# First layer's mixer projections as single fp32 products, and the log steps of the state space laid out as one run per partition

## The chip, the cores and the metric

The kernel runs on one core of a Trainium2 chip. The metric is the device time of one execution in microseconds, the median over runs. Its work is spread over TensorE (PE in the profile; PEld is its weight load), VectorE (DVE), ScalarE (ACT), GpSimd (POOL) and the DMA queues, one of which is fed by SyncE (SP).

## The reference

Two layers over 512 tokens of width 1024. Each layer is a mixer and an expert stage:

```python
xn = rms_norm(h, norm1_g[l])
proj = xn @ w_in[l]                       # 1024 x 2056: u, q, k, v (512 each), f (8)
y_ssm = s5_mixer(u, lambda, log_dt, b, c, ...)     # 32 groups of 64 complex states
y_att = fox_attention(q, k, v, f + fox_b[l])
h = h + concat(rms_norm(y_ssm), rms_norm(y_att)) @ w_o[l]
h = h + peer_ffn(rms_norm(h, norm2_g[l]), ...)     # top 16 of 16384 experts, 8 heads
```

In `s5_mixer`, `dt = exp(log_dt)` has one value per group (32 per layer), and from it, lambda, b and c come the tables of the scan. All of it is float32.

## The kernel before

Tokens lie in 4 blocks of 128 (TB), the width in 8 blocks of 128 (KD). A program order is written in Python; a scheduler with a timeline of its own then puts the instructions of each engine in a fixed order, and buffers and semaphores are derived from that. So a change in one place may move others.

**Projections.** `norm_T` (L239) normalises each token block, transposes it on PE (L256) and writes it in two parts: `x1`, rounded to fp32r by ACT (L259), and the rest `x2` by DVE (L260). `stream` (L178) loads blocks of `w_in` of 512 KB on SP's queue into 5 buffers called `raw` (L157) and `wsplit` (L161) splits each the same way: `hi` on ACT (L166), `lo` on POOL or DVE (L167). `mm3` (L198) then forms a product as three fp32r matmuls: hi x1, hi x2, lo x1 (L200 to L202). `proj_T` (L211) does that for a 128-column block of weights: two halves of 256 tokens, 8 steps of k each. In the mixer there are 13 such blocks (4 for u, 1 for f, 4 for q, 4 for k) and then v, with the weights as the moving operand of 512 columns: 32 products. In the first layer `lo` is made on POOL for the blocks with `i % 4 != 3` and on DVE for the rest and for v.

**Tables of the scan.** `s5_prep` (L265) loads lambda, `log_dt`, b, c and d on SP's queue (L279 to L291), takes the exponential of `log_dt` on ACT (L293), and works out sines and cosines (L304 to L323), powers (L328 to L333, L378 to L380), and for each of four groups of heads three tables, with transposes (L459) and small products (L471) on PE, and part of the work on POOL. They go out to DRAM (`s5p`, L415, L438, L462, L482) and come back in `s5` (L586). For the first layer this runs at the start, between the projections. For the second it is woven into the first layer's expert stage: its loads stand in SP's queue between those of expert weights.

**Scan, attention, output.** `s5` (L570) runs four groups: products L594, DVE work L600 to L621, products L625 to L627, a GELU on ACT, transposes L633. Then come the gate (`glu`, first product L644), attention (L677 to L691) and the output projection.

**Expert stage.** Norm, routing and gate tables; then 116 of 128 blocks of expert weights `peer_uT` are loaded, split and multiplied as above (`u_stage`), with results stored to DRAM (`ad`); then the second tables. Near the start of the u blocks, ACT's queue also loads gates (`g<-gd`) and results (`ar<-ad`) ahead.

The lines of `s5_prep` that load the log steps, and their host side (L1090):

```python
bass.AP(tensor=ld.tensor, offset=ld.offset + l * 2 * NPR + g, ap=[[0, 64], [2, NPR]])   # NPR = 16
o["log_dt"] = c(f("ssm_log_dt"))
```

Each of two loads fills 64 partitions with the same 16 values, read from every second element.

Of the kernel before, what the change touches and what calls it, by code (L numbers as in the profile page):

```python
# [9 lines left out]
F32R = mybir.dt.float32r  # L10
# [3 lines left out]
AF = mybir.ActivationFunctionType  # L14
OP = mybir.AluOpType
# [4 lines left out]
L, S, D = 2, 512, 1024  # L20
TB = S // 128
KD = D // 128
NPR = 16
# [21 lines left out]
class Net:  # L45
# [136 lines left out]
    def stream_rest(s, specs, depth, ahead, raws):  # L182
        out = {}
        n = len(specs)

        def fetch(i):
            for k in range(i, min(i + ahead, n)):
                if k not in raws:
                    raws[k] = s.wload(*specs[k][:2])
            for k in range(i, min(i + depth, n)):  # L190
                if k not in out:
                    out[k] = s.wsplit(raws[k], specs[k][2] if len(specs[k]) > 2 else False)

        for i in range(n):
            fetch(i)
            yield out.pop(i)
# [14 lines left out]
    def proj_T(s, p, wh, wl):  # L211

        for hf in range(2):
            po = s.toks(p[:, 256 * hf:256 * hf + 256])
            for k in range(KD):
                bs = slice(2 * hf, 2 * hf + 2)
                s.mm3(po, wh[:, k], wl[:, k], s.x1[:, bs, k], s.x2[:, bs, k], k == 0, k == 7)


# [16 lines left out]
        nc.vector.reciprocal(r, q)  # L236
        return r

    def norm_T(s, gain, gb, xt, pt, order=range(TB)):  # L239

        nc = s.nc
        nc.scalar.dma_start(gb, bass.AP(tensor=gain.tensor, offset=gain.offset + s.l * D, ap=[[0, 128], [1, D]]))
        x1 = s.k("x1", [TB, KD, 128], F32R)
        x2 = s.k("x2", [TB, KD, 128], F32R)
        for b in order:
            ssq = s.k("ssq", [16], bufs=4)
            xn = s.t(xt, [D], bufs=2) if xt else s.k("raw", [1024], bufs=5)
            with s.tc.high_priority(offset=NORM):
                nc.scalar.activation(xn, s.h[:, b], AF.Square, accum_out=ssq[:, 0:1])
                r = s.rstd(ssq[:, 0:1], 1, D)  # L250
                s.normed = s.sqrt
                s.scaled = nc.vector.scalar_tensor_tensor(xn, s.h[:, b], r, gb, op0=OP.mult, op1=OP.mult)
            for q in range(2):
                p = s.p(pt)
                for k in range(4):
                    nc.tensor.transpose(p[:, k * 128:(k + 1) * 128], xn[:, (4 * q + k) * 128:(4 * q + k + 1) * 128],  # L256
                                        s.ident)
                pk = p.rearrange("p (k t) -> p k t", k=4)
                nc.scalar.activation(x1[:, b, 4 * q:4 * q + 4], pk, AF.Copy)  # L259
                nc.vector.tensor_tensor(x2[:, b, 4 * q:4 * q + 4], pk, x1[:, b, 4 * q:4 * q + 4], op=OP.subtract)  # L260
        s.x1, s.x2 = x1, x2
        return xn


    def s5_prep(s, l, engs, ptag, bufs):  # L265

        nc, a = s.nc, s.a
# [6 lines left out]
        def new():  # L274
            idx[0] += 1
            return sm[:, idx[0] - 1]
# [4 lines left out]
        ld = a["log_dt"]  # L281
        for g in range(2):
            nc.sync.dma_start(dt[g * 64:(g + 1) * 64],
                              bass.AP(tensor=ld.tensor, offset=ld.offset + l * 2 * NPR + g,
                                      ap=[[0, 64], [2, NPR]]))
        bc = s.t("pbc", [4, NPR, 16])
        for i, n in enumerate(("b_re", "b_im", "c_re", "c_im")):
            nc.sync.dma_start(bc[:, i], a[n][l])
# [69 lines left out]
        nr, q = new(), new()  # L358
# [127 lines left out]
    def mixer(s):  # L486
        nc, a, l = s.nc, s.a, s.l
# [1 line left out]

        qa = [s.t(f"q{i}", [2, S]) for i in range(4)]  # L490
        wv = a["w_in"][l].rearrange("(k p) c -> p k c", p=128)
        specs = [(wv[:, :, 128 * cb:128 * cb + 128], [8, 128], l == 0 and i % 4 != 3)
                 for i, cb in enumerate(list(range(0, 4)) + [16] + list(range(4, 12)))]
        specs += [(wv[:, 2 * i:2 * i + 2, 1536:2048], [2, 512]) for i in range(4)]
        ws = s.stream(specs, pre=2)
        if l == 0:
            early = s.phase("prep")
# [1 line left out]
            prep = s.s5_prep(0, (nc.vector, nc.gpsimd), "pt", 2)  # L499
            next(prep)  # L500
            s.sb = s.mix
        s.norm_T(a["norm1_g"], s.k("hn", [D]), None, "pt", (3, 0, 1, 2) if l else range(TB))
        if l == 0:
            s.small_loads()
        x1, x2 = s.x1, s.x2

        us = []
        for qd in range(4):
            wh, wl = next(ws)
# [13 lines left out]
        wh, wl = next(ws)  # L523
# [19 lines left out]
        with s.phase("s5"):  # L543
            s.s5(us, gT)
            ka = [s.tm(f"k{i}", [2, S]) for i in range(4)]
            for i in range(4):
                nc.gpsimd.memset(ka[i][64:66], 1.0)
                nc.scalar.dma_start(ka[i][65:66], f0[2 * i:2 * i + 2])
            for cb in range(4):
                wh, wl = next(ws)  # L550
                p = s.p("pj")
                s.proj_T(p, wh, wl)
                for hh in range(2):
                    nc.scalar.activation(qa[cb][0:64, hh], p[64 * hh:64 * hh + 64], AF.Copy, scale=0.125)
            for cb in range(4):
                wh, wl = next(ws)
                p = s.p("pj")
                s.proj_T(p, wh, wl)
                for hh in range(2):
                    v.tensor_copy(ka[cb][0:64, hh], p[64 * hh:64 * hh + 64])  # L560
            vv = s.tm("v", [TB, 512])
            pv = [s.p("pj") for _ in range(4)]
            for i in range(4):
                wh, wl = next(ws)
                for kk in range(2):
                    k = 2 * i + kk
                    for b in range(4):
                        s.mm3(pv[b], x1[:, b, k], x2[:, b, k], wh[:, kk], wl[:, kk], k == 0, k == 7)
            for b in range(4):
                s.evac(vv[:, b], pv[b])  # L570
        with s.phase("att"):
            s.glu(gT)
            op = s.out_proj()
# [497 lines left out]
def layout(inp):  # L1071

    import numpy as np
    c = np.ascontiguousarray
    f = lambda n: np.asarray(inp[n])
    o = {}
# [10 lines left out]
    o["fox_b"] = c(f("fox_b_f").T)  # L1087
    st = lambda n: c(f(n).reshape(L, 16, 2, 64).transpose(0, 2, 3, 1).reshape(L, 128, 16))
    o["lam_re"], o["lam_im"] = st("ssm_lambda_re"), st("ssm_lambda_im")
    o["log_dt"] = c(f("ssm_log_dt"))  # L1090
    sb = lambda n: c(f(n).reshape(L, 16, 2, 64, 16).transpose(0, 2, 3, 1, 4).reshape(L, 128, 16, 16))
    o["b_re"], o["b_im"] = sb("ssm_b_re"), sb("ssm_b_im")
    sc = lambda n: c(f(n).reshape(L, 16, 2, 16, 64).transpose(0, 2, 4, 1, 3).reshape(L, 128, 16, 16))
# [36 lines left out]
```

## Time and profile before

| what | us |
|---|---|
| median of 3 runs | 3337.83 (3333.64 to 3341.49) |
| the profiled execution | 3333.71 |
| its span | 3331.9 |
| TensorE busy | 3068.3 (92% of the span) |
| VectorE / GpSimd / ScalarE busy | 2607.7 / 1630.1 / 1450.8 |
| mean granted TensorE clock | 0.962 of full speed |

The span runs from the first to the last instruction; the rest of the execution's own time, 1.8 us, lies outside it. Times in the rows are counted from the span's start. Matmuls are pipelined: the time of one in a row is from its start to its end, and what it costs in a stream is the step from one start to the next. An fp32 matmul of the program stands as two PE instructions in the trace. The first layer's mixer runs from 0 to about 321 us, its expert stage to about 1730; the second layer follows in the same way.

### The profile page before, as it was taken

How to read it: one execution, taken by the hardware profiler on the slowest of the kernel's cores; microseconds unless marked ns; L12 is line 12 of the kernel's file. 1: busy time of each engine (PE TensorE's matmuls, PEld its weight loads, DVE VectorE, ACT ScalarE, POOL GpSimd, SP SyncE). 2: the span in 40 equal slices, each digit the busy share in tenths (PEclk: the TensorE clock that was granted, in tenths of full speed). 3: DMA queues.
4: the chain of work that ended last, by engine and by line, in shares of the span. 5: the costliest groups of instructions: out<-in, count | busy, mean ns of one | idle time of the engine just before them, and what ended most of it. 6: DMA issues, size and time to landing. Idle time of an engine off the chain costs nothing.

```text
span 3331.9 us, 45931 instructions
## 1 busy us (share of the span) xinstructions
PE 3068.3 (92%) x16418; PEld 2708.6 (81%) x16418; DVE 2607.7 (78%) x4907; ACT 1450.8 (44%) x2591; POOL 1630.1 (49%) x890
## 2 busy tenths in 40 slices
PE   6889988899979998999999999888999999999998
PEld 5856978888969877778879669878989998788887
DVE  7775699988745789888877556999886658888887
ACT  3344322378823343333343433334887333333333
POOL 3400276656569555454420003766756884544452
PEclk8989988899989999999999999889999999999999
DMA  5612276657778988999974123766767999899996
GB/s 153 216 44 64 100 246 227 212 217 277 261 247 293 335 313 306 315 335 336 321 239 145 51 64 114 248 221 210 260 245 280 306 311 332 308 354 340 339 337 217
DMA packets 395446, 811.12 MB, mean 243 GB/s; under 512 B 30768, under 2 KB 236592, under 8 KB 392144
## 3 DMA queue, kind: packets, MB, share of 16 engines
q1 hardware_dynamic: 140448, 326.23, 28.6%
q0 software_dynamic: 73728, 268.47, 22.8%
q10 hardware_dynamic: 181040, 213.48, 19.1%
q8 instruction: 129, 2.11, 0.3%
q14 instruction: 101, 0.83, 0.1%
HBM read 693.19 MB, written 114.82 MB: 243 GB/s over the span
## 4 chain that ended last, share of the span: by engine, by line
PE 50%; DVE 22%; issue 9%; DMA 8%; ACT 3%; POOL 2%; ACTq 1%; POOLq 0%; DVEq 0%; SPq 0%
PE pb L908 15%; PE pc L908 7%; DMA ru<-in_peer_u_dram,idx 6%; PE pa L202 3%; PE pa L200 3%; PE pa L201 3%; DVE ru L932 2%; DVE t L862 2%; DVE h L935 2%; PE pb L872 2%; PE pc L202 2%; PE pc L200 2%; PE pc L201 2%; DVE t L817 2%; DVE lo L167 1%
## 5 line engine op out<-in xcount | busy, mean ns | idle before, releaser
L167 POOL TENSOR_TENSOR lo<-raw,hi 128x1024 fp32r<-128x1024 f32 x306 | 822.0, 2693 | 940.4 <-ACT hi L166 898.0
L166 ACT ACTIVATE hi<-raw 128x1024 fp32r<-128x1024 f32 x578 | 610.2, 1057 | 683.8 <-issue 167.4
L908 PE MATMUL pb<-hi,cc 128*128 128x512 f32 x2048 | 608.2, 399 | 16.9 <-DVE cc L898 9.1
L932 DVE SCALAR_TENSOR_TENSOR ru<-ru,hn 128x1024 f32<-128x1024 f32 x256 | 393.7, 1539 | 209.3 <-DMA ru<-in_peer_u_dram,idx 209.1
L908 PEld LDWEIGHTS pb<-hi,cc 128*128 128x128 f32 x2048 | 386.2, 190 | 111.9 <-DVE cc L898 12.4
L167 DVE TENSOR_TENSOR lo<-raw,hi 128x1024 fp32r<-128x1024 f32 x272 | 337.9, 1244 | 128.8 <-ACT hi L166 126.2
L921 POOL DMA_INDIRECT rv<-in_peer_v_dram,idx x256 | 372.3, 1454 | 129.6 <-issue 49.2
L921 POOL DMA_INDIRECT ru<-in_peer_u_dram,idx x256 | 384.0, 1500 | 91.3 <-DVE ru L932 31.3
L202 PE MATMUL pa<-x,lo 128*128 128x384 f32 x1120 | 389.4, 348 | 17.1 <-POOL lo L167 16.5
L200 PE MATMUL pa<-x,hi 128*128 128x384 f32 x1120 | 388.4, 347 | 11.8 <-ACT hi L166 11.7
L201 PE MATMUL pa<-x,hi 128*128 128x384 f32 x1120 | 387.2, 346 | 0.0
L935 DVE SCALAR_TENSOR_TENSOR h<-rv,gc,h 128x1024 f32<-128x1024 f32 x256 | 377.2, 1473 | 10.0 <-DMA rv<-in_peer_v_dram,idx 5.2
L200 PE MATMUL pc<-x,hi 128*128 128x384 f32 x928 | 327.3, 353 | 32.2 <-ACT hi L166 32.2
L202 PE MATMUL pc<-x,lo 128*128 128x384 f32 x928 | 326.7, 352 | 16.8 <-POOL lo L167 16.6
L908 PE MATMUL pb<-lo,cc 128*128 128x512 f32 x1024 | 325.5, 399 | 9.9 <-DVE lo L167 9.8
L201 PE MATMUL pc<-x,hi 128*128 128x384 f32 x928 | 324.7, 350 | 0.0
L908 PE MATMUL pc<-hi,cc 128*128 128x512 f32 x1024 | 323.9, 397 | 0.0
L933 ACT ACTIVATE gc<-gc 128x1 f32<-128x1 f32 x256 | 51.4, 201 | 527.6 <-DVE ru L932 451.7
L862 DVE TENSOR_TENSOR t<-io,idt 128x2048 f32<-128x2048 f32 x96 | 259.5, 2713 | 5.7 <-PE pb L872 5.6
L872 PE MATMUL pb<-small,t 128*128 128x128 f32 x1536 | 221.8, 288 | 36.0 <-ACT small L866 21.5
L872 PEld LDWEIGHTS pb<-small,t 128*128 128x128 f32 x1536 | 210.5, 198 | 48.6 <-ACT small L866 30.6
L897 ACT ACTIVATE cc<-c 128x384 fp32r<-128x384 f32 x256 | 132.9, 519 | 254.8 <-DVE c L895 191.2
(329 smaller groups left out, 5974.4 us busy)
## 6 DMA issues: line engine op xcount, KB each, us to landing
raw<-in_peer_uT_dram SPq DMA_DIRECT2D x256, 512.0 KB
raw<-in_peer_v_dram SPq DMA_DIRECT2D x256, 512.0 KB
gd<-t ACTq DMA_DIRECT2D x24, 2048.0 KB
g<-gd ACTq DMA_DIRECT2D x64, 768.0 KB
ad<-ao ACTq DMA_DIRECT2D x232, 192.0 KB
ar<-ad ACTq DMA_DIRECT2D x58, 768.0 KB
raw<-in_w_in_dram SPq DMA_DIRECT2D x34, 512.0 KB
s5p<-pE ACTq DMA_DIRECT2D x16, 512.0 KB
```

What stands on the lines that cost most here:

```text
L166: s.nc.scalar.activation(hi, raw, AF.Copy)
L167: ins = eng.tensor_tensor(lo, raw, hi, op=OP.subtract)
L200: mm(ps, lh, rh, start=start, stop=False)
L201: mm(ps, lh, rl, start=False, stop=False)
L202: mm(ps, ll, rh, start=False, stop=stop)
L862: v.tensor_tensor(oh, s.iota[:, None, None, :].to_broadcast([128, 2, 8, 128]), idT[:, 0:2, t0:t0 + 8, None].to_broadcast([128, 2, 8, 128]) ...
L872: nc.tensor.matmul(p[:, t], oh[:, 1, 4 * f + t], o2[:, 4 * f + t], start=True, stop=True)
L897: on_act = nc.scalar.activation(ch, c[:, 0], AF.Copy)
L908: s.nc.tensor.matmul(s.pv[tb][hf], x[:, sl], y[:, 512 * hf:512 * hf + 512], start=(first and e == 0), stop=(last and e == 2))
L921: nc.gpsimd.indirect_dma_start(out=o, out_offset=None, in_=a[n], in_offset=off)
L932: v.scalar_tensor_tensor(ru, ru, 1.0, s.hn, op0=OP.mult, op1=OP.mult, accum_out=c[:, 0:1])
L935: v.scalar_tensor_tensor(acc, rv, c[:, 2:3], acc, op0=OP.mult, op1=OP.add)
```

## The change

In the first layer the weights of the mixer's projections and the normalised tokens are no longer split. `stream` hands out the raw weight buffer itself when the third entry of a spec is None, `norm_T` with `split=False` writes one fp32 tile on ACT, and the products are single fp32 matmuls. The second layer, the output projection and the expert stage keep the split. And `log_dt` is transposed on the host, so that each partition reads 16 values that lie next to each other (64 bytes).

```diff
@@ stream_rest
-                    out[k] = s.wsplit(raws[k], specs[k][2] if len(specs[k]) > 2 else False)
+                    how = specs[k][2] if len(specs[k]) > 2 else False
+                    out[k] = (s.view(*raws.pop(k)), None) if how is None else s.wsplit(raws[k], how)
@@ proj_T
+                if wl is None:
+                    s.nc.tensor.matmul(po, wh[:, k], s.x[:, bs, k], start=(k == 0), stop=(k == 7))
+                    continue
                 s.mm3(po, wh[:, k], wl[:, k], s.x1[:, bs, k], s.x2[:, bs, k], k == 0, k == 7)
@@ norm_T
-                nc.scalar.activation(x1[:, b, 4 * q:4 * q + 4], pk, AF.Copy)
-                nc.vector.tensor_tensor(x2[:, b, 4 * q:4 * q + 4], pk, x1[:, b, 4 * q:4 * q + 4], op=OP.subtract)
+                if split:
+                    ...
+                else:
+                    nc.scalar.activation(s.x[:, b, ks], pk, AF.Copy)
@@ s5_prep
-                              bass.AP(tensor=ld.tensor, offset=ld.offset + l * 2 * NPR + g,
-                                      ap=[[0, 64], [2, NPR]]))
+                              bass.AP(tensor=ld.tensor, offset=ld.offset + (2 * l + g) * NPR,
+                                      ap=[[0, 64], [1, NPR]]))
@@ mixer
-        specs = [(wv[:, :, 128 * cb:128 * cb + 128], [8, 128], l == 0 and i % 4 != 3)
-                 for i, cb in enumerate(list(range(0, 4)) + [16] + list(range(4, 12)))]
-        specs += [(wv[:, 2 * i:2 * i + 2, 1536:2048], [2, 512]) for i in range(4)]
+        how = False if l else None
+        specs = [(wv[:, :, 128 * cb:128 * cb + 128], [8, 128], how) for cb in [0, 1, 2, 3, 16] + list(range(4, 12))]
+        specs += [(wv[:, 2 * i:2 * i + 2, 1536:2048], [2, 512], how) for i in range(4)]
@@ mixer, v
-                        s.mm3(pv[b], x1[:, b, k], x2[:, b, k], wh[:, kk], wl[:, kk], k == 0, k == 7)
+                        if wl is None:
+                            nc.tensor.matmul(pv[b], s.x[:, b, k], wh[:, kk], start=(k == 0), stop=(k == 7))
+                        else:
+                            s.mm3(pv[b], s.x1[:, b, k], s.x2[:, b, k], wh[:, kk], wl[:, kk], k == 0, k == 7)
@@ layout
-    o["log_dt"] = c(f("ssm_log_dt"))
+    o["log_dt"] = c(f("ssm_log_dt").reshape(L, NPR, 2).transpose(0, 2, 1))
```

The scheduler orders the first layer's mixer anew. Behind it the engines' orders are as before but for a few neighbours that change places.

On PE before, the scan's first products (L594, `wb` is a table that came back from DRAM, `u` the first projection) stand behind all 13 projection blocks and part of v (`pj` written from `hi` and `lo` with 512 columns):

```order
L202 MATMUL pj_1756<-hi_1759,x_26_125 128x512
L200 MATMUL pj_1753<-hi_1759,x_25_124 128x512
L201 MATMUL pj_1753<-lo_1760,x_25_124 128x512
L202 MATMUL pj_1753<-hi_1759,x_26_125 128x512
L200 MATMUL pj_1754<-hi_1759,x_25_124 128x512
L201 MATMUL pj_1754<-lo_1760,x_25_124 128x512
L202 MATMUL pj_1754<-hi_1759,x_26_125 128x512
L594 MATMUL p_161_1034<-u_287,wb_1028 128x128
L594 MATMUL p_162_1035<-u_287,wb_1028 128x128
```

On PE now (the same products are L607, a projection is L219) they stand inside the last two blocks of k:

```order
L219 MATMUL pj_1210<-x_25_124,raw_1166 128x256 x16
L219 MATMUL pj_1231<-x_25_124,raw_1187 128x256 x7
L607 MATMUL p_148_841<-u_238,wb_835 128x128
L607 MATMUL p_149_842<-u_238,wb_835 128x128
...
L219 MATMUL pj_1231<-x_25_124,raw_1187 128x256 x9
L219 MATMUL pj_1252<-x_25_124,raw_1208 128x256 x5
L607 MATMUL p_162_905<-u_266,wb_899 128x128
```

Ahead of the first L594 there were 208 products of projections and 14 products of v; ahead of the first L607 there are 183 products, and the other 25 and nearly all of v come between the scan's groups.

On ACT before, at the start, the splits (`hi`) stand between the copies of the transposed tokens (`x`) and the exponential of the log steps (L293, `psm` is the tile of the small vectors):

```order
L166 ACTIVATE hi_228<-raw_99 128x1024
L234 ACTIVATE rs_q_203<-rs_m_201 128x1
L259 ACTIVATE x_25_124<-pt_160 128x512
L166 ACTIVATE hi_232<-raw_101 128x1024
L259 ACTIVATE x_25_124<-pt_167 128x512
L293 ACT_TABLE_LOAD
L293 ACTIVATE psm_107<-psm_107 128x16
L259 ACTIVATE x_25_124<-pt_184 128x512
L166 ACTIVATE hi_296<-raw_226 128x1024
L296 ACTIVATE psm_107<-psm_107 128x16
```

On ACT now (L272 is the copy, L304 the exponential):

```order
L272 ACTIVATE x_25_124<-pt_157 128x512
L238 ACTIVATE rs_q_196<-rs_m_194 128x1
L272 ACTIVATE x_25_124<-pt_163 128x512
L304 ACT_TABLE_LOAD
L304 ACTIVATE psm_107<-psm_107 128x16
L307 ACTIVATE psm_107<-psm_107 128x16
L323 ACT_TABLE_LOAD
L323 ACTIVATE psm_107<-psm_107 128x16 x2
L272 ACTIVATE x_25_124<-pt_179 128x512
```

The splits are gone, and the copies of the last two token blocks stand behind both sines (L323).

## Rows read from the trace of the kernel before

**Rows 1.** Page, part 2: PE busy in tenths, 40 slices of 83.3 us.

```profile
PE   6889988899979998999999999888999999999998
```

**Rows 2.** Windows, first layer: us, then busy us (count) per engine, clock, DMA.

```profile
15.60:33.50 17.90, 4.45 (x19) 3.91 (x19) 3.67 (x8) 2.71 (x3) 5.52 (x2) 0.71 0.13 30
33.50:150.40 116.90, 100.49 (x759) 97.30 (x760) 91.97 (x256) 42.71 (x83) 56.43 (x47) 0.94 0.62 192
150.40:202.50 52.10, 42.50 (x243) 37.62 (x243) 44.75 (x87) 10.71 (x13) 0.34 (x3) 0.84 0.38 127
```

**Rows 3.** Timeline of ACT: start us, us, instruction, idle before it and its end.

```profile
32.22 1.28 ACT L293 ACT_TABLE_LOAD   x1 [15.19 <-DMA psm<-in_log_dt_dram]
```

**Rows 4.** DMA packets between 14 and 30 us.

```profile
DMA packets 1701, 0.01 MB, mean 0 GB/s; under 512 B 1701, under 2 KB 1701, under 8 KB 1701
```

**Rows 5.** Timeline of PE: start us, us, instruction; two neighbours each time.

```profile
17.50 0.41 PE L200 MATMUL pj<-x,hi 128*128 128x256 f32 x1
17.71 0.41 PE L201 MATMUL pj<-x,hi 128*128 128x256 f32 x1
...
134.56 0.28 PE L200 MATMUL pj<-x,hi 128*128 128x256 f32 x1
134.68 0.28 PE L201 MATMUL pj<-x,hi 128*128 128x256 f32 x1
...
140.70 0.39 PE L200 MATMUL pj<-hi,x 128*128 128x512 f32 x1
140.93 0.39 PE L201 MATMUL pj<-lo,x 128*128 128x512 f32 x1
```

**Rows 6.** Chain of waits, 0 to 420 us: start us, us, group.

```profile
124.54 1.70 PE pt L471 x16
...
150.62 1.57 PE p L594 x14
...
202.73 6.87 PE pt L644 x16
```

**Rows 7.** Groups by line, 0 to 202.5: count | busy us, mean ns.

```profile
L167 POOL TENSOR_TENSOR lo<-raw,hi 128x1024 fp32r<-128x1024 f32 x10 | 28.6, 2864 | 33.7 <-ACT hi L166 24.8 <-ACT rs_q L234 8.8
...
L167 DVE TENSOR_TENSOR lo<-raw,hi 128x1024 fp32r<-128x1024 f32 x10 | 12.7, 1269 | 5.9 <-ACT hi L166 5.5 <-issue 0.4
...
L166 ACT ACTIVATE hi<-raw 128x1024 fp32r<-128x1024 f32 x20 | 21.1, 1056 | 43.0 <-PE pj L202 16.5 <-DVE pEa L378 10.3 <-PE pj L201 7.3
```

**Rows 8.** Timeline of DVE and POOL, 40 to 90 us.

```profile
40.67 0.83 DVE L318 TENSOR_TENSOR psm<-psm 128x16 f32<-128x16 f32 x1 [3.12 <-ACT psm L312]
...
82.18 0.67 DVE L425 TENSOR_TENSOR pP<-pT,half 128x512 f32<-128x512 f32 x1
...
84.35 4.48 POOL L167 TENSOR_TENSOR lo<-raw,hi 128x1024 fp32r<-128x1024 f32 x1 [5.73 <-ACT hi L166]
...
86.55 2.82 DVE L425 TENSOR_TENSOR pP<-pT,half 128x512 f32<-128x512 f32 x1
```

**Rows 9.** Windows, expert stage: first layer, and the same place in the second.

```profile
930.00:966.00 36.00, 12.20 (x53) 10.55 (x51) 7.78 (x8) 6.98 (x12) 9.47 (x5) 0.70 0.56 186
...
2588.00:2624.00 36.00, 30.41 (x158) 29.78 (x157) 27.65 (x22) 14.99 (x25) 29.57 (x16) 0.91 0.93 318
```

**Rows 10.** Timeline of the SP queue, 921 to 961 us.

```profile
921.89 7.95 SPq L283 DMA_DIRECT2D psm<-in_log_dt_dram  x2
...
935.16 3.16 SPq L157 DMA_DIRECT2D raw<-in_peer_uT_dram  x1
...
960.36 0.86 SPq L157 DMA_DIRECT2D raw<-in_peer_uT_dram  x2
```

**Rows 11.** Waits, PE (906 to 970), SP (915 to 965): total, times, longest.

```profile
PE pc L200 <- ACT hi L166: 20.8, 2, 12.4
...
SPq L288 <- DMA g<-gd: 9.1, 1, 9.1
...
SPq L288 <- DMA ar<-ad: 7.2, 1, 7.2
```

More of the change, by code (lines that the diff above doesn't have):

```diff
@@ L187, in fetch @@
             for k in range(i, min(i + ahead, n)):
-                if k not in raws:
+                if k not in raws and k not in out:
                     raws[k] = s.wload(*specs[k][:2])
@@ L237, in rstd, with norm_T @@
         return r
-    def norm_T(s, gain, gb, xt, pt, order=range(TB)):
+    def norm_T(s, gain, gb, xt, pt, order=range(TB), split=True):
         nc = s.nc
         nc.scalar.dma_start(gb, bass.AP(tensor=gain.tensor, offset=gain.offset + s.l * D, ap=[[0, 128], [1, D]]))
-        x1 = s.k("x1", [TB, KD, 128], F32R)
-        x2 = s.k("x2", [TB, KD, 128], F32R)
+        if split:
+            s.x1 = s.k("x1", [TB, KD, 128], F32R)
+            s.x2 = s.k("x2", [TB, KD, 128], F32R)
+        else:
+            s.x = s.k("x1", [TB, KD, 128])
         for b in order:
@@ L258, in norm_T @@
                 pk = p.rearrange("p (k t) -> p k t", k=4)
-                nc.scalar.activation(x1[:, b, 4 * q:4 * q + 4], pk, AF.Copy)
-                nc.vector.tensor_tensor(x2[:, b, 4 * q:4 * q + 4], pk, x1[:, b, 4 * q:4 * q + 4], op=OP.subtract)
-        s.x1, s.x2 = x1, x2
+                ks = slice(4 * q, 4 * q + 4)
+                if split:
+                    nc.scalar.activation(s.x1[:, b, ks], pk, AF.Copy)
+                    nc.vector.tensor_tensor(s.x2[:, b, ks], pk, s.x1[:, b, ks], op=OP.subtract)
+                else:
+                    nc.scalar.activation(s.x[:, b, ks], pk, AF.Copy)
         return xn
@@ L501, in mixer @@
             s.sb = s.mix
-        s.norm_T(a["norm1_g"], s.k("hn", [D]), None, "pt", (3, 0, 1, 2) if l else range(TB))
+        s.norm_T(a["norm1_g"], s.k("hn", [D]), None, "pt", (3, 0, 1, 2) if l else range(TB), split=l > 0)
         if l == 0:
             s.small_loads()
-        x1, x2 = s.x1, s.x2
         us = []
@@ L567, in mixer @@
                     for b in range(4):
-                        s.mm3(pv[b], x1[:, b, k], x2[:, b, k], wh[:, kk], wl[:, kk], k == 0, k == 7)
+                        if wl is None:
+                            nc.tensor.matmul(pv[b], s.x[:, b, k], wh[:, kk], start=(k == 0), stop=(k == 7))
+                        else:
+                            s.mm3(pv[b], s.x1[:, b, k], s.x2[:, b, k], wh[:, kk], wl[:, kk], k == 0, k == 7)
             for b in range(4):
```

## The prediction

> **What bounds the kernel now.** I read the page's slices first: TensorE (PE) is at 8 or 9 tenths nearly everywhere, so what can be won lies where its row dips: slices 1 to 3, and slice 12 (916 to 1000 us) [rows 1]. Both are places that the change touches, so I went there.
>
> At the start the table of stretches shows PE busy 4.45 of the 17.9 us from 15.6 to 33.5, and DVE 3.67 [rows 2]. ACT's timeline says why: 15.19 us in one wait for the load of `log_dt`, ended at 32.22 [rows 3]. ACT works in order, so the copies of the last two token blocks wait behind the exponential, and PE behind these. The DMA view shows what the load is: 1701 packets, 0.01 MB in all, in 16 us, 106 per us [rows 4]. Two loads of 64 partitions by 16 single values are 2048 packets of 4 bytes, 19 us at that rate, and the other loads of SP's queue stand behind them.
>
> From 33.5 to 150.4 no engine is full: PE 100.49 of 116.9, DVE 91.97 [rows 2]. The bound there is the table work, in which DVE, POOL, PE and ACT wait for each other. DVE also stretches when POOL is at a `lo`: the same L425 on DVE takes 0.67 us alone and 2.82 beside the `lo` that POOL runs from 84.35 to 88.83 [rows 8]. From 150.4 to 202.5 the scan is DVE's (44.75 of 52.1) [rows 2].
>
> The dip in the expert stage is 930 to 966: PE busy 12.20 of 36 us at a mean clock of 0.70; at the same place in the second layer, with the same gate loads but without the table loads, 30.41 of 36 at 0.91 [rows 9]. PE waits 20.8 us there for splits of weights [rows 11] whose loads come late: SP issues one at 935.16 and the next two at 960.36, with the log-step loads (921.89, 7.95 us) ahead and the other table loads around them [rows 10].
>
> **The products in fp32: what PE pays.** Step from start to start at full clock: 0.12 us for an fp32r matmul of 256 columns, 0.23 for 512 [rows 5]; so three cost 0.36 and 0.69. A plain fp32 product is two PE instructions; 16 of 512 columns take 6.87 us, 0.429 each [rows 6]. That is 0.859 for a product of v, and by columns 0.43 for one of 256 (an estimate; the form does not occur in a stream). 208 products pay 0.07 more, 14.6 us, and 32 of v 0.17, 5.4: PE gets 20 us more work.
>
> **What the splits give back.** Ten `lo` on POOL (28.6 us), 7 of 10 on DVE (1.27 each, 8.9 us; the other 3 are the output projection's), 17 of 20 `hi` on ACT (1.06 each, 18 us) [rows 7], and the eight subtractions for `x2` on DVE. Each POOL `lo` also cost DVE about 2 us, the 2.82 against 0.67 above. Three lie between DVE's first sine product at 40.67 and the first finished `pP` at 82.18 [rows 8]: of these 41.5 us some 10 go (6.4 of stretch, 2.5 for two `lo` on DVE, the rest for three `x2`).
>
> **So who is last in the new first stage?** With the log steps there at about 16, the sines follow some 5 us later (an estimate: the 8.5 from 32.22 to 40.67 without the `hi` on ACT and the `x2` on DVE that sat between), and the first `pP` at 21 + 31 = 52. In the new order PE has 80 products before it needs that: 15 + 80 x 0.43 = 49, plus 1.7 for transposes and 2.2 for the half clock at the start (the step at 17.5 is 0.21 for 256 columns, twice that at 134.56 [rows 5]), gives 53. They meet. From there a group of tables is some ten DVE operations of 0.67 us and as many short ones, 8 to 10 us (an estimate from the order), and PE has 22 products and 24 small instructions beside each, 12 us. PE becomes the bound of the whole stage, and I sum it from PE alone:
>
> - 208 x 0.43 = 89.4 and 32 x 0.859 = 27.5;
> - 288 small fp32 instructions (64 L471, 32 L459, 64 L594, 96 L625 to L627, 16 L633, 16 transposes of tokens) at 0.11 (1.70/16 and 1.57/14 [rows 6]) = 31.7;
> - together 148.6. Start at 15, half clock 2.2, waits around the first two groups 3.5: the stage's end is at 169.
>
> Now the first product of the gate (L644) starts at 202.7 [rows 6]. That is 33 us; for waits that such a count doesn't see I take 2 off: **31 us**. In the scan PE now has 25 x 0.43 + 27.5 + 19.4 = 58 us where DVE has some 41, so PE is the bound there also; it stays busy, and the half clock that this stretch has now (0.84 in the mean [rows 2]) should go.
>
> Bounds: if the freed time of POOL, DVE and ACT is worth just what PE pays, only the start's wait is left, 15 us. If PE never waits, 36. Weight loads now hold a `raw` buffer until PE is through with it, so loads run at most 5 blocks ahead; a block is 6.9 us of PE, a load of 512 KB is well inside that, and I cost it at nothing; if a block did wait, each microsecond would count. The table reads stand in SP's queue behind the second load of v, which waits for PE to leave the first k block, 23 products or 10 us before their first use: hidden.
>
> The fp32 product costs 0.859/0.69 = 1.24 times three fp32r ones by the rows. The Trainium skill's "FP8 and Floating Point Precision" (TensorE Precision Notes) counts four passes for true fp32, 4/3 of three. By it a product would cost 0.48 and 0.92, 12 us more than I take, and the time would be near 3300. The trace has its own duration for the 512-column form, and I go by that.
>
> **The log steps in the expert stage.** The new loads are 128 runs of 64 bytes; at 106 packets per us that is 1.2 us in place of 19 and more. But the rest of the chain stays: SP's loads of b and c wait 9.1 us for the gate load `g<-gd` and 7.2 for `ar<-ad` on ACT's queue [rows 11]. These ran beside the 4-byte packets, and in the second layer they run without them. So the bounds are: 4 us, if the gate loads stay as slow and only the first weight load moves, by half of the log steps' 7.95; and 21, if the stretch becomes the second layer's, with 18.2 more busy us in 36 [rows 9] and its clock. I take the second layer's busy time, the nearest row, less 1 for the table loads that still stand in SP's queue: **17 us**.
>
> **Sum.** 3333.7 (the profiled execution) - 31 - 17 = 3285.7. The median of the runs stands 4.1 above that execution; I take half: **3288**. All edits behind are ordered as before, and the rest has no fixed point in time, so it shifts.
>
> **Rivals.**
> 1. The gate loads, not the log steps, hold the weights in the expert stage: 4 us there. For: SP's longest waits name them. Against: the same loads in the second layer leave PE 30.41 of 36. 3333.7 - 31 - 4 + 2 = 3301.
> 2. PE's extra 20 us eat what the splits give back; 15 at the start stays. For: PE is busy 86% from 33.5 on. Against: DVE's stretches. 3333.7 - 15 - 17 + 2 = 3304.
> 3. fp32 at 4/3 of three fp32r products: 3300. For: no stream of the 256-column form is in the trace.
> 4. The log steps load no faster, since 64 bytes are still short runs: the start and the expert stage stay, and only the splits' 16 us are won: 3320. Against: packets go by number in [rows 4], and there are 16 times fewer.
> 5. Slower: the projection stream runs at 1.2 GHz (granted clock 0.5) instead of 2.4. Place: 15 to 110 us, where PE was idle and at half clock before (0.71 in the mean from 15.6 to 33.5 [rows 2]). Each product then costs double, 117 us if all do; it decides from 48/117, 41% of the products, and at two thirds the time is 3366. Against: the clock was back once PE was busy (0.94 after 33.5), and the new stream has fewer gaps.
>
> **How the numbers follow.** Forecast 0.62, rival 1 0.11, rival 2 0.12, rival 3 0.06, rival 4 0.05, rival 5 0.04. The gains at the ends of the bounds are 36 + 21 = 57 and 15 + 4 = 19: 3277 and 3315; with the spread of the runs (8) below and the 4 above, the range is 3269 to 3319. It holds all but rival 5 and part of rival 4. 0.2% of this time is 6.7 us, about what a measurement can tell from no change. The first four cases are faster: 0.93; a part of rival 5 and mixtures near no gain: 0.03 the same; 0.04 slower.
>
> **What would show it.** Right: ACT's wait for `log_dt` gone and the sines near 21; L219 pairs 0.43 apart; PE above 9 tenths from 20 to 169 with the first L644 of the new kernel (there L657) at about 170; in the expert stage PE busy over 25 of the 36 us that begin 24 us behind the last product of the gate tables (L872, now L885). Wrong: PE waiting for `pP` or for `raw` loads in 60 to 110; a step of L219 over 0.24; SP standing still between two weight loads of the expert stage for 20 us again.

## The result and the profile after

The changed kernel takes **3297.2 us** (median of 4 runs, 3288.5 to 3303.1), the kernel before beside it 3335.7 (4 runs); the ratio is 0.9888, 95% interval 0.9865 to 0.9910. The forecast was 3288 in a range of 3269 to 3319: 48 us of gain stood in its sum, 38.5 came. The profiled execution took 3299.4 us (span 3297.6), 34.3 less than that of before.

PE's busy share by slices, the answer to [rows 1], with the clock that it was granted:

```profile
PE   8999987889999998999999999878999999999998
...
PEclk9999989999999999999999999889999999999999
```

Slices 1 to 3 went from 6, 8, 8 to 8, 9, 9, slice 12 (it begins near 907 us here) from 7 to 9. Slice 7 (495 to 577 us), which the change does not touch, went from 8 to 7. The stretches that answer to [rows 2] and [rows 9] (us, then busy us and count of PE, PEld, DVE, ACT, POOL, then clock, DMA share, GB/s):

```profile
15.60:33.50 17.90, 17.90 (x93) 15.87 (x92) 17.48 (x118) 5.15 (x11) 6.21 (x8) 1.00 0.34 90
33.50:118.00 84.50, 77.36 (x382) 67.56 (x381) 48.83 (x129) 24.16 (x60) 25.34 (x31) 0.94 0.61 198
118.00:177.20 59.20, 59.20 (x300) 42.27 (x299) 47.85 (x90) 10.15 (x12) 0.34 (x3) 1.00 0.53 172
915.00:951.00 36.00, 29.98 (x152) 29.11 (x151) 24.74 (x17) 12.60 (x20) 26.11 (x14) 0.86 0.93 313
```

PE is busy without a gap where it had 4.45 of 17.9 us, and through the whole scan; DVE fell to 58% between. In the expert stage 24 us behind the last gate product it is busy 29.98 of 36 us, for 12.20. ACT's timeline shows that the wait of [rows 3] is gone (start, length, instruction):

```profile
14.82 1.28 ACT L304 ACT_TABLE_LOAD   x1
...
17.06 1.28 ACT L323 ACT_TABLE_LOAD   x1
19.02 0.52 ACT L323 ACTIVATE psm<-psm 128x16 f32<-128x16 f32 x2 [0.67 <-DVE psm L322]
```

The table load for the exponential starts at 14.8 us and the sines at 19.0. PE's timeline gives the price of a product and the three places where PE still stood:

```profile
25.20 20.02 PE L219 MATMUL pj<-x,raw 128*128 128x256 f32 x92
...
52.87 0.66 PE L470 MATMUL pt<-ident,pP 128*128 128x128 f32 x4 [1.60 <-DVE pP L436]
53.36 5.78 PE L219 MATMUL pj<-x,raw 128*128 128x256 f32 x26
62.85 3.62 PE L482 MATMUL pt<-pC,pP 128*128 128x32 f32 x16 [3.72 <-ACT pT L472]
66.29 9.01 PE L219 MATMUL pj<-x,raw 128*128 128x256 f32 x28
...
102.22 0.66 PE L470 MATMUL pt<-ident,pP 128*128 128x128 f32 x4 [1.57 <-ACT pW L492]
```

92 instructions in 20.0 us are 0.217 each, two per product: 0.43, as estimated. The 28 from 66.29 take 0.32 each: from the end of the wait of 3.72 on, the granted clock was half for 10.2 us (61.6 to 71.8).

### The profile page after: what moved, and what is told of

It is laid out like the page before. It is cut to its first block, busy times and chain, and to the rows that moved or that the text cites. A ratio compares the mean times of both kernels' runs of the same rounds, so it can differ in the third digit from the quotient of the medians.

```text
span 3297.6 us, 45399 instructions
## 1 busy us (share of the span) xinstructions
PE 3074.1 (93%) x16178; PEld 2687.6 (82%) x16178; DVE 2602.4 (79%) x4892; ACT 1432.4 (43%) x2574; POOL 1589.3 (48%) x880
## 5 line engine op out<-in xcount | busy, mean ns | idle before, releaser
L167 POOL TENSOR_TENSOR lo<-raw,hi 128x1024 fp32r<-128x1024 f32 x296 | 792.8, 2686 | 890.7 <-ACT hi L166 828.5
L166 ACT ACTIVATE hi<-raw 128x1024 fp32r<-128x1024 f32 x561 | 591.9, 1057 | 602.0 <-issue 157.6
L945 DVE SCALAR_TENSOR_TENSOR ru<-ru,hn 128x1024 f32<-128x1024 f32 x256 | 378.1, 1478 | 204.0 <-DMA ru<-in_peer_u_dram,idx 204.0
L921 PEld LDWEIGHTS pb<-hi,cc 128*128 128x128 f32 x2048 | 383.9, 189 | 115.2 <-DVE cc L911 16.6
L167 DVE TENSOR_TENSOR lo<-raw,hi 128x1024 fp32r<-128x1024 f32 x265 | 328.6, 1241 | 127.4 <-ACT hi L166 127.2
L948 DVE SCALAR_TENSOR_TENSOR h<-rv,gc,h 128x1024 f32<-128x1024 f32 x256 | 404.4, 1580 | 8.2 <-DMA rv<-in_peer_v_dram,idx 5.9
L203 PE MATMUL pa<-x,lo 128*128 128x384 f32 x1120 | 387.2, 346 | 17.2 <-POOL lo L167 16.6
L921 PE MATMUL pb<-lo,cc 128*128 128x512 f32 x1024 | 324.8, 398 | 13.2 <-DVE lo L167 11.4
```

The costliest lines, as they stand in the source:

```text
L166: s.nc.scalar.activation(hi, raw, AF.Copy)
L167: ins = eng.tensor_tensor(lo, raw, hi, op=OP.subtract)
L203: mm(ps, ll, rh, start=False, stop=stop)
L921: s.nc.tensor.matmul(s.pv[tb][hf], x[:, sl], y[:, 512 * hf:512 * hf + 512], start=(first and e == 0), stop=(last and e == 2))
L945: v.scalar_tensor_tensor(ru, ru, 1.0, s.hn, op0=OP.mult, op1=OP.mult, accum_out=c[:, 0:1])
L948: v.scalar_tensor_tensor(acc, rv, c[:, 2:3], acc, op0=OP.mult, op1=OP.add)
```

## The experiments

Every one was timed beside the kernel before on the same chip; a ratio is to that. "The mark" is the first transpose of the second norm, at 323.2 us before and 302.7 after: the first piece behind the first layer's mixer. "The u stage" runs from the last gate product (906.3 us before, 891.2 after) to the first product with the gated values, `pb<-hi,cc` (1095.2 and 1060.1).

By these points the 34.3 us between the two profiled executions lie so: 20.5 up to the mark and 20.0 in the u stage; the stretch from the mark to the u stage, which the change leaves alone, took 5 us more (588.5 for 583.1), and all behind the u stage 1 us more. That stretch took 580 to 589 us in the executions of this record, so its 5 us tell nothing.

**1. The log steps alone** (the splits stay):

```
-  offset=ld.offset + l * 2 * NPR + g,   ap=[[0, 64], [2, NPR]]
+  offset=ld.offset + (2 * l + g) * NPR, ap=[[0, 64], [1, NPR]]
```

> The kernel before with the log steps laid out as runs of 16 values, in both layers; the splits stay. Theory (two gains that add up: about 15 us at the start from the log steps, about 10 more in the first stage from the splits, about 20 in the expert stage from the log steps): the first gate product starts near 188 us (202.8 before, 177.3 after), the expert stage keeps its 20, and the time is about 35 below before, near 3301. Rival, the log steps bring all of the first stage too and the plain products pay just what they give back: first gate product near 177 and a time as after, near 3297 or lower. Rival, without the freed splits the tables are no earlier: first gate product near 200, time near 3315.

Measured: 3294.9 us, ratio 0.9884 (0.9864 to 0.9905). That is as much as the whole change brings. The parts of the trace are as the theory has them, first gate product at 189.0, mark at 309.4, u stage 170.4 us; the time is 6 below its 3301.

**2. The plain products alone** (the log steps are read as 2048 packets again).

> The kernel after with the log steps read as 2048 packets of 4 bytes again, in both layers; the projections stay plain. Theory (the terms add up): ACT waits for the log steps until about 32 us again, the first gate product starts near 192 us (10 us before that of the kernel before), the expert stage has its 24 us of idle PE again, and the time is about 10 below before, near 3326. Rival, PE's 20 us eat all that the splits give back: no change, 3330 to 3342. Rival, the missing splits leave PE so little to do in front of the tables that the late tables cost more than before: the first gate product after 203 and a time above before.

Measured: 3331.0 us, ratio 0.9990 (0.9978 to 1.0002): no gain that can be told from none, and the time is the rival's (3330 to 3342). The trace is nearer to the theory: first gate product at 194.1, mark at 316.4. The stretch from 0 to the mark in four kernels, first before, then the log steps alone, the plain products alone, and both (columns as above, the second number is PE's busy time):

```profile
0.00:323.20 323.20, 266.45 (x1514) 211.72 (x1515) 220.14 (x535) 127.74 (x245) 68.36 (x64) 0.94 0.38 120
```

```profile
0.00:309.40 309.40, 268.89 (x1514) 213.92 (x1515) 224.89 (x535) 127.91 (x245) 67.89 (x64) 0.94 0.40 125
```

```profile
0.00:316.40 316.40, 277.81 (x1274) 200.36 (x1275) 194.24 (x520) 110.67 (x228) 37.34 (x54) 0.97 0.39 122
```

```profile
0.00:302.70 302.70, 279.55 (x1274) 202.13 (x1275) 193.50 (x520) 110.84 (x228) 37.46 (x54) 0.97 0.40 128
```

The parts add up here: the log steps bring 13.8 and 13.7 us (323.2 to 309.4, 316.4 to 302.7), the plain products 6.8 and 6.7. The plain products do it so: PE's idle time (length less busy) falls by 18.2 and 17.4 us, and its busy time rises by 11.4 and 10.7. Busy time at half clock counted by half, it rises by 17 to 19; the rest is the clock, 0.97 for 0.94. So what idle PE gave back paid for the products and no more; the 7 us that are left are clock. Other executions bear the size out: beside the new log steps the mark stood at 300.0 to 302.7 in three kernels with plain products (after, that of 5, and after placed in 9) and at 308.5 to 310.4 in three with splits (that of 1 and two of 9). In the time these 7 us do not show; the interval of this run reaches from 7 us less to 1 us more than before, so they are not excluded either.

Where PE waited in the kernel of 1 up to its first gate product (total us, times, longest):

```profile
PE pt L625 <- DVE ss L618: 7.2, 3, 2.9
PE pt L459 <- DVE pP L425: 5.7, 3, 2.7
```

The former is the scan's DVE work, with 0.8 more for `L626`; PE's waits there for its own `hi` and `lo` are 5.6 us. In after neither is among PE's waits, and that for `pP` is 1.6: there PE has projections to do between the scan's groups, in the order shown ahead of the prediction. So a good part of the idle time went with the new order, not with the engines' time.

The plain kernel with the old log steps also shows a second hold at the start, in PE's timeline:

```profile
21.30 2.32 PE L219 MATMUL pj<-x,raw 128*128 128x256 f32 x10
38.31 4.63 PE L219 MATMUL pj<-x,raw 128*128 128x256 f32 x10 [14.69 <-DMA raw<-in_w_in_dram]
```

PE waits 14.69 us, and for weights, not for ACT: the third weight load stands behind the other table loads in SP's queue, which issued it at 33.86 (at 17.10 in after). The 4-byte packets held the start in two ways at once.

**3. The log steps of the second layer alone**, which are read in the first layer's expert stage. The edit is that of 1 for `l == 1`, the kernel before otherwise.

> The kernel before with the log steps laid out as runs for the second layer's load alone, which is read in the expert stage of the first layer; the first stage stays as it was. Theory (the 4-byte packets hold SP's queue and slow the gate loads on ACT's queue): PE's idle time in the first layer's products of u falls from 24 us to about 6, the stage from 188.9 us to about 169, the time to about 3316. Rival (the gate loads hold the weights by themselves, and the gain in the kernel after came from its shifted phase): the stage falls by 4 to 8 us, and the time is near 3330.

Measured: 3312.5 us, ratio 0.9929 (0.9909 to 0.9948); u stage 172.2 us. The stretch of the u products, before and here:

```profile
906.30:1095.20 188.90, 164.89 (x908) 163.20 (x907) 95.95 (x86) 59.55 (x98) 144.73 (x76) 0.93 0.83 280
```

```profile
912.90:1085.10 172.20, 164.66 (x908) 163.01 (x907) 91.03 (x84) 59.45 (x98) 145.83 (x76) 0.97 0.91 307
```

PE's idle time falls from 24.0 to 7.5 us. By the medians 17.6 are left for the start (39.5 - 21.9, each good to some 7 us); the mark of 1 gave 13.8. So the gain of the log steps is in its two places. This run also shows how far one execution can be trusted: up to 906 us it does the work of the kernel before, yet its mark was at 329.9, since 13.7 us at half clock fell behind the first gate product, where before had none.

**4. What in the packets does the harm?** The kernel before, with the second layer's log steps, laid out as before, issued on POOL's queue.

```
-  nc.sync.dma_start(dt[g * 64:(g + 1) * 64],
+  (nc.gpsimd if l else nc.sync).dma_start(dt[g * 64:(g + 1) * 64],
```

> The kernel before with one change: the second layer's log steps, still 2048 packets of 4 bytes and read in the expert stage of the first layer, are issued on POOL's queue and not on SP's. Theory A (SP stands still for the 7.95 us of the issue and the weight loads are behind it): the weights come as with the new layout, the stage of the u products takes near 172 us (188.9 before), the time is near 3313. Theory B (the packets themselves slow the gate loads that SP waits for, whatever queue they are in): the stage stays at 183 to 190 us and the time at 3326 to 3336.

Measured: 3336.2 us, ratio 1.0029 (1.0012 to 1.0045), u stage 191.6 us: theory B, both just above its ranges. The DMA view of this kernel from 923 to 945 us (busy tenths, GB/s in 40 pieces of 0.55 us, packets, queues):

```profile
DMA  9999999000900009099919990900000111333458
GB/s 344 349 365 393 216 87 30 7 20 3 0 0 20 0 7 21 13 21 36 80 75 28 23 0 0 0 20 26 25 22 30 49 60 65 114 126 139 164 205 312
...
q0 software_dynamic: 180, 0.42, 77.6%
q10 hardware_dynamic: 1081, 0.89, 12.2%
q1 hardware_dynamic: 264, 0.61, 7.7%
```

POOL's queue (q0) takes 77.6% of the 16 DMA engines' time and moves 0.42 MB; from 926 to 938 us hardly anything else moves. SP is free of the 7.95 us of issuing and waits 17.9 us for the load of results `ar<-ad` instead. So the harm is not in SP's issuing.

But on POOL's queue the load is not 2048 packets. The trace has it as 32 packets of 256 bytes, 64 values each, and one takes 8.0 us in the mean; the rest of q0 is gathered rows of 4 KB at 0.17 us and a few packets of 4 bytes. What the packets do on SP's queue must be read from the kernel before itself, here from 928 to 934 us, and below it the same place of the stage in the kernel of 3 (934.6 to 940.6 us):

```profile
DMA packets 1174, 0.68 MB, mean 114 GB/s; under 512 B 597, under 2 KB 1174, under 8 KB 1174
...
q10 hardware_dynamic: 592, 0.68, 38.2%
q1 hardware_dynamic: 582, 0.00, 4.5%
```

```profile
DMA packets 2146, 2.09 MB, mean 348 GB/s; under 512 B 95, under 2 KB 1982, under 8 KB 2146
...
q10 hardware_dynamic: 1916, 1.41, 81.3%
```

With the 4-byte packets on SP's queue (q1), ACT's queue (q10), which carries the gates and results, gets 592 packets through in 6 us, as many as q1; without them 1916 (0.68 and 1.41 MB). The DMA engines are what is shared, not the queue. That agrees with the Trainium skill, "DMA: Bandwidth & Descriptors" (Queues, rings and completion order), where an engine serves its queues in turn, one packet at a time. The near equal counts, 592 and 582, fit it in these 6 us; from 934 to 942 us ACT's queue gets more than q1.

The busy share hides this: the 582 packets are booked with 4.5% of the engines' time. What a value costs an engine can only be estimated: 0.15 us from the start, where 106 per us went through, if all 16 engines took part [rows 4], and 0.13 from POOL's queue (8.0 us for 64).

**5. Plain products in the second layer too.**

```
-  how = False if l else None
+  how = None
```

> The kernel after with the plain products in the second layer's mixer too. There the tables are long done, and PE was busy over 9 tenths. Theory (208 products pay 0.07 us each and 32 of v 0.17): the second layer's stage from the first product to the first gate product takes up to 20 us longer than after, less what PE idled there for splits, and the time is 10 to 20 above after, 3307 to 3317. Rival, true fp32 at 4/3 of three fp32r products: 32 us longer. Rival, the splits hold PE there too: no longer than after, within 4 us of 3297.

Measured: 3307.9 us, ratio 0.9917 (0.9888 to 0.9945), 11 above after by the medians; the two intervals overlap, so the stage has to show it. From the expert stage's last product to the second layer's first gate product, after and here:

```profile
1693.40:1828.10 134.70, 128.53 (x942) 121.79 (x941) 84.23 (x137) 43.92 (x60) 4.14 (x7) 0.96 0.53 157
```

```profile
1690.40:1838.50 148.10, 145.17 (x702) 116.27 (x701) 61.15 (x112) 28.02 (x44) 4.13 (x7) 1.00 0.46 136
```

13.4 us longer: busy time rises by 16.6 (20.8 with the clock set aside), idle falls by 3.2. The price of 20 us was right, and 4/3 of three fp32r products (32 us) is not what a plain product costs here.

**6. The splits kept as dead work beside the plain products.** Nothing reads the halves.

```
   if how is None:
+      s.wsplit(raws[k], k < 13 and k % 4 != 3)
       out[k] = (s.view(*raws.pop(k)), None)
```

> The kernel after, with plain products, but the weights of the first layer's mixer are split all the same, on the engines that did it before; nothing reads the halves. Theory (the splits cost because they take DVE, ACT and POOL from the tables): PE's idle time up to the second norm goes from 23 us back to 35 to 42, that norm's first transpose starts at 314 to 322 (302.7 after), and the time is 10 to 18 above after. Rival (PE waited for its own split operands, and the plain product frees it of that wait alone): idle near 23, the transpose at 300 to 306, and the time as after.

Measured: ratio 0.9937 (0.9918 to 0.9957), some 16 us above after; mark at 310.3, PE idle 31.3 us up to it (23.2 after). So 8 of the 17 us of idle time come back with the engines' work, less than the theory had. PE's waits up to the gate product, in this kernel and in after (total us, times, longest):

```profile
PE pt L474 <- DVE pP L440: 11.5, 7, 4.8
```

```profile
PE pt L470 <- DVE pP L436: 1.6, 1, 1.6
```

It is the tables that come late. The other half does not come back: neither the scan's waits (0.9 us here, 8.0 in the kernel of 1, see 2) nor those of the products for their own halves (5.6 there). The subtractions for `x2` were not put back here; how much each of these makes is not told apart. The trace shows 8 of the 16 us; this profiled execution was 9.5 below its kernel's median.

**7. Every `lo` on DVE, none on POOL** (log steps as in 1, splits kept): `l == 0 and i % 4 != 3` becomes `False`.

> The kernel with the log steps as runs and the splits kept, every low part on DVE and none on POOL. My reason for the splits' price was that a low part on POOL (28.6 us for ten) stretches DVE's table work, about 2 us each, against 1.27 us if DVE does it itself. Theory: DVE's 0.67 us operations keep that time, the tables come some 5 us earlier, and the second norm's first transpose starts near 304 us (309.4 with POOL). Rival (the stretch is small in sum, or falls where PE does not wait): DVE gets 9 to 12 us more work ahead of the tables, and that transpose starts at 315 to 320, the time 3 to 10 above 3295.

Measured: 3292.7 us, ratio 0.9882 (0.9851 to 0.9913), no change from 1; first gate product at 184.6 (189.0 in the kernel of 1), mark at 308.2. At the gate product the theory's 5 us are there; behind it this execution had 6.8 us at half clock and that of 1 had none, so that 1.2 are left at the mark, between theory and rival. DVE's groups up to the gate product, with ten `lo` on POOL (the kernel of 1), then with none:

```profile
L167 DVE TENSOR_TENSOR lo<-raw,hi 128x1024 fp32r<-128x1024 f32 x10 | 12.5, 1245 | 6.8 <-ACT hi L166 6.4 <-issue 0.4
...
L378 DVE TENSOR_TENSOR pE<-pEa,pEb 128x512 f32<-128x512 f32 x8 | 10.7, 1363 | 5.1 <-DMA s5p<-pE 5.1
```

```profile
L167 DVE TENSOR_TENSOR lo<-raw,hi 128x1024 fp32r<-128x1024 f32 x20 | 25.2, 1259 | 16.7 <-ACT hi L166 16.6
...
L378 DVE TENSOR_TENSOR pE<-pEa,pEb 128x512 f32<-128x512 f32 x8 | 5.9, 775 | 0.7 <-DMA s5p<-pE 0.7
```

The stretch is real: 1363 ns with POOL's `lo` beside it, 775 without (777 after). The Trainium skill, "SBUF — State Buffer" (SBUF: two separate sides), has DVE operations with two SBUF inputs and POOL's reads take one pair of ports in turn; the rows agree. In sum it is more than these eight operations: DVE's busy time up to the mark falls from 224.9 to 217.3 us although it has 12.7 us more `lo` to do, so some 20 us of stretch went (an estimate from these sums). But PE's wait for `pP` only falls from 5.7 to 5.2 us: most of what DVE gains is not where PE waits.

**8. Plain products for u and the forget gate alone**, 80 in place of 240; the tokens are split after them, and q, k and v take the three fp32r products.

```
+  s.x = [s.k(t, [KD, 128], bufs=3) for t in ("hi", "hi", "lo", "lo")]
...
+  (wv[:, :, 128 * cb:128 * cb + 128], [8, 128], how if i < 5 else l == 0 and i % 4 != 3)
```

> The kernel after with plain products only in the five blocks that come before the tables are there (u and the forget gate, 80 products of 256 columns, here as 160 of 128); the tokens are split after them, and q, k and v go in three fp32r products again. Theory (PE is the bound of the first stage, and a plain product costs it 0.07 or 0.17 more): PE's work up to the second norm falls by 13 to 15 us against after, idle rises by less, that norm's first transpose starts at 292 to 298 (302.7 after, 309.4 with all splits), and the time is 5 to 10 below after, near 3290. Rival (what the splits take from DVE, ACT and POOL comes back as idle PE, as it did when they were removed: 17 us of work for 17 us of idle): the transpose at 303 to 309, and the time within 4 us of 3296.

Measured: **3276.7 us, ratio 0.9841 (0.9813 to 0.9869)**, the best of all. But the mark was at 300.1, 2.6 before that of after, with PE busy 263.3 us and idle 36.8: between the ranges of theory and rival, with the rival's account, since PE's work falls by 13.5 us (half clock set aside) and its idle time rises by 13.6. Most of the gain lay where nothing was changed: the 512-column products of the expert stage stepped 227 ns, not 232. What I knew to be different there was where `hi` and `lo` lie in SBUF.

**9. The place of `hi` and `lo`.** Three kernels with the same instructions in the same order, only allocated otherwise: after, the kernel of 1, and the kernel of 8 with the tokens first; then the kernel of 1 shifted by 128 bytes.

```
+  for t in ("hi", "lo"):
+      for _ in range(3):
+          s.k(t, [1024], F32R, bufs=3)
```

> The kernel after, instruction for instruction; only the place of the hi and lo buffers in SBUF is other (they are allocated ahead of the tokens, and begin at byte 59,872 of a partition instead of 93,792). In the kernel with plain products for u alone, where they lie there too, the 512-column products of the expert stage stepped 227 ns, against 232 in all other kernels. Theory (the place of the buffers sets that step): 227 ns here, about 10 us less PE work in each layer's last stage, and the time 18 to 24 below after, 3273 to 3279. Rival (something else of that kernel, such as where its instructions lie, does it): 232 ns and the time as after, 3291 to 3303.

> The kernel with the log steps as runs and all splits kept, with the hi and lo buffers placed as in the run before this one and nothing else changed. Theory: as there, 18 to 24 below the same kernel without it, 3271 to 3277. On the plain products: if they bring nothing beside the log steps, this run and the one before it are within 4 us; if they do, this one is 5 or more slower. Rival on the place: 3289 to 3301.

> The kernel with plain products for u and the forget gate alone, with the tokens allocated first, so that the hi and lo buffers lie at byte 92,640 and up; the instructions and their order are the same. Theory (of the 20 us by which that kernel was below after, 2.6 came from its first stage and the rest from the step of 227 ns): the step is 232 ns again, the second norm's first transpose stays near 300 us, and the time is 3290 to 3298, within 6 of after. Rival (the mixed form is worth the 15 to 20 by itself): near 3277 to 3282.

> The kernel with the log steps as runs and all splits kept, with 128 bytes left free ahead of the hi and lo buffers, so that they begin at byte 93,920 of a partition and not at 93,792; instructions and order are the same. The expert stage's 512-column products stepped 232 ns with hi at 93,792 and at 77,408, and 227 ns with hi at 59,872 and at 92,640: the former two leave 96 when divided by 256, the latter two 224, and so does the new place. Theory (that remainder sets the step): 227 ns, PE's work in the first layer's stage of the v products near 585 us (596 without the shift), the time 8 to 18 below 3295. Rival (another property of the place, which the four cannot tell apart): 232 ns, work near 596, the time as without the shift, 3288 to 3302.

| kernel | `hi` begins at | step | us | ratio |
|---|---|---|---|---|
| after, placed | 59,872 | 227 | 3286.7 | 0.9861 (0.9838 to 0.9885) |
| log steps, placed | 59,872 | 227 | 3285.1 | 0.9873 (0.9845 to 0.9901) |
| plain u, tokens first | 92,640 | 227 | 3285.0 | 0.9843 (0.9819 to 0.9867) |
| log steps, 128 bytes on | 93,920 | 232 | 3297.4 | 0.9888 (0.9870 to 0.9905) |

The step is read from one start to the next. In after and in after placed, 22 products lie between these two starts, 5.11 and 4.99 us:

```profile
1199.73 0.63 PE L921 MATMUL pc<-hi,cc 128*128 128x512 f32 x2
...
1204.84 0.64 PE L921 MATMUL pb<-lo,cc 128*128 128x512 f32 x2
```

```profile
1199.73 0.62 PE L925 MATMUL pc<-hi,cc 128*128 128x512 f32 x2
...
1204.72 0.61 PE L925 MATMUL pb<-lo,cc 128*128 128x512 f32 x2
```

The place does set the step: after and the kernel of 1 changed it with nothing but the allocation changed. My rule for it (the remainder of `hi` by 256) fell by the shift, which gave 232. But the shift was no clean test. The 128 bytes stand ahead of every buffer allocated later, so `cc`, the operand that these products move against the weights, went from byte 174,816 to 174,944 with them; in the other kernels of this table, in after and in that of 6 it lies at 174,816. From `hi` to `cc` it is a multiple of 256 bytes in both places with 227 ns (59,872 and 92,640), and 128 are left over in all three with 232 (77,408, 93,792, and 93,920 after the shift). So the distance by 256 fits every place, and no run has tested it by moving `cc` alone.

The placing brought some 9 us to after, half of what I expected and within overlapping intervals (0.9861 and 0.9888), though PE's busy time fell by 9 in each layer: the second layer's last stage took 601.1 us for 598.7, and PE idled 23.9 for 12.6 (DMA 0.91 busy, 0.90 without). The kernel of 8 had 227 ns at its other place too, so its run without that step is still missing; that it keeps 6 us over after placed (0.9843 and 0.9861) is within the intervals.

On the plain products these runs say what 1 and 2 said. With and without them beside the new log steps: 0.9888 and 0.9884, 0.9888 (the shifted kernel), placed 0.9861 and 0.9873. No difference is shown, in either direction; a few us stay open.

## Why the prediction was right, and where it was not

The time fell in the range and on the right side, but one step failed. That it fell in the range says little: the range also held rivals 1, 2 and 3 (3301, 3304, 3300), and 3297.2 is nearer to each of them than to 3288.

- **The step that failed: "What the splits give back."** Of the stage's 31 us, 15 were the start's wait and 16 what the freed engines would give over PE's price. Up to the first gate product, where the forecast was made, 25.5 us came (202.8 to 177.3); at the mark it is 20.5 us, of which 6.7 come with the plain products, and these are clock; in the time they do not show (0.9990 alone). The change gave 17 to 18 us of idle PE, and PE's price took 17 to 19. I counted the freed time on DVE (some 10 us before the first `pP`), found that PE would be the bound, and did not then compare two sums of PE's own: idle before, work added. Rival 2 said just that, at 0.12; on this term it was right. Even of the idle time that went, only 8 us come back when the splits do (experiment 6).
- **The stage's end.** 177.3 us, not 169. Waits of PE were 6.9 us (1.60, 3.72 and one of 1.6 at 101) for the 3.5 I took, and 10.2 us of half clock at the longest, some 5 us lost (an estimate: half of them), I had not priced; the 2.2 of half clock at the start that I had priced did not come (1.00 from 15.6 to 33.5). The half clock of the scan went, as forecast. The first gate product also was a poor mark: from it to the second norm the stage took 5 us more than before (125.4 for 120.4), with 6.8 us of it at half clock, where before had none.
- **The log steps at the start.** Right in cause and near in size: 13.8 at the mark, 17.6 as what the medians leave (39.5 - 21.9), for 15. The rows of before let me see ACT's wait; the weight loads behind the same packets I mentioned and gave no price.
- **The log steps in the expert stage.** 17 forecast; 20.0 in the stage with the whole change; done alone, 16.7 in the stage and 21.9 in the time (interval 17 to 30). Rival 1 (4 us) falls: the gate loads were slow because of the packets. The issue still takes 7.49 us and SP still waits for `g<-gd` in it, but the weights come:

```profile
907.12 0.33 SPq L157 DMA_DIRECT2D raw<-in_peer_uT_dram  x1
907.50 7.49 SPq L294 DMA_DIRECT2D psm<-in_log_dt_dram  x2
...
916.88 0.33 SPq L157 DMA_DIRECT2D raw<-in_peer_uT_dram  x1
...
928.42 21.08 SPq L157 DMA_DIRECT2D raw<-in_peer_uT_dram  x7
```

  That is SP's timeline of after; in [rows 10] the second load behind the log steps came at 960.36, 38 us after them, here at 928.42, 21 after.
- **The other rivals.** 3 (4/3 of three fp32r products) falls by the step of 0.217 us, 0.43 for a product against 3 x 0.12, and by experiment 5. The count of four passes does not fall with it: 0.43 us at 2.4 GHz are some 4.1 cycles for each of 256 columns, and the 0.12 of an fp32r matmul are 1.1 (estimates from the steps). By these an fp32r matmul costs more than a cycle per column, and the ratio is 1.2 and not 4/3. 4 falls by ACT's wait; 5 by the clock, 1.00 from 15.6 to 33.5 and half for only 10.2 us of the stage.

So the sum was 15 + 16 + 17, where the traces have 13.8 + 6.7 + 20.0, with 6 us lost where nothing was changed, and the medians of the runs done alone about 17.6 + 0 + 21.9.

## What to carry to other kernels

Before trading vector work for matmul work, set the idle time of PE in that stage against the matmul time added: freed engines can return at most the former, and here what they returned (17 to 18 us) was what was added. A load of single values costs twice over, by what waits for it and by the loads of other queues that are in flight beside it, so it can be worth a layout of its own even where nothing waits for it. The busy share of the DMA engines does not show this cost; counting packets by queue does. And when a variant wins, look whether it wins where it was changed; when a shift is to test a place, look what else it shifts.

## What the runs showed of the hardware that I had not expected

- 4-byte packets on one queue slow the others while the engines look idle: in 6 us ACT's queue got 592 packets through beside 582 of 4 bytes, 1916 without them, and the 582 were booked with 4.5% of the engines' time.
- The same 8 KB on POOL's queue went as 32 packets of 64 values, 8.0 us each, and in 22 us 87 GB/s were moved at 0.98 busy.
- The same matmuls stepped 227 or 232 ns by the place of their weights' buffers: 227 with `hi` at 59,872 and 92,640, 232 at 77,408 (the kernel of 6), 93,792 and 93,920. The distance to `cc` by 256 fits them all, untested; why is open.
- PE's half clock falls differently from execution to execution: the same work took 120.4 or 126.9 us behind the first gate product (0 or 13.7 us at half clock). So a single profiled stage tells no difference below some 7 us; that takes several executions.
